# Where weights lie against the moving operand modulo 256 bytes, and 512-column projections by column halves, in an fp32 encoder layer

## Chip, cores and metric

One NeuronCore of one Trainium2 chip. The metric is the device time of one execution in microseconds; the kernel before has a median of 2016.3 us over three runs (2015.68 to 2016.89).

## What is computed

One post-norm layer of a bidirectional encoder over 512 tokens of width 2048, all in float32:

```
h  = layer_norm(x)
z  = h @ w_in                         # 2048 x 3136: latents c_q, c_kv, k_pe, and x_lru, g_lru
ya = attention of 8 heads from the latents (w_uq, w_ukv, rotary, softmax over 512 keys)
yl = gelu(g_lru) * bidirectional RG-LRU(conv(x_lru))     # gates: 8 blocks x 4 products 128x128
h  = layer_norm(alpha*h + concat(ya, yl) @ w_out)        # 2048 x 2048
h  = layer_norm(alpha*h + relu(h @ w_up)^2 @ w_down)     # 2048 x 8192, 8192 x 2048
```

## The kernel before, in words

Activations lie with features on the partitions and the 512 tokens along the free axis. Every fp32 product is made of three fp32r matmuls: weight and activation are each split into a high part (rounded to fp32r, on ACT) and the rest (a subtraction on DVE), and PE adds `wh·xh`, `wh·xl` and `wl·xh` into one PSUM bank. Such a triple is the unit of all that follows. Each matmul loads its 128x128 stationary operand (the weights) while the matmul ahead of it streams its moving operand (the activations): in the trace a `wh·xh` starts at 100.08 us and the load for the matmul behind it at 100.09. So while `wh·xh` streams, `wh` is loaded again; while `wh·xl` streams, `wl` is loaded; while `wl·xh` streams, the next `wh` is loaded.

**Stages in order of time.** The input projections (22 of 25 column tiles by `linear`, L128, each over 16 k-tiles), with the RG-LRU blocks (`lru_block`, L397) between them; attention (`proj`, `q_pe`, `v_pair`, `scores`, `weighted`); the output projection (14 of 16 column tiles by `linear`); the up projection; the down projection. `linear` and the gates of `lru_block` use `mm3` (L123): three matmuls of 512 columns.

**Up and down.** Nearly all of both is `winograd` (L832): seven products (`product`, L816) instead of eight, each of 8 triples of 256 columns, with weights that `wsplit` splits (hi and lo). Its operands are eight blocks of half the tokens: B11, B21, B22, X4, T1, T2, T3 (high part `..h`, rest `..l`). `classic` with `mm_blocks` (L699) does nine column tiles without that scheme, by halves of 256 columns.

**Where weights lie.** `wtile` (L104) makes a slot of 1024 + `WPAD` words, and weights begin `woff` words into it:

```
    WPAD = 32
    woff = [16]
        t = p.tile([P, 1024 + WPAD], F32R, tag=tag, name=tag, bufs=bufs)
        return t[:, woff[0]:woff[0] + 1024]
```

There are three high slots and two low ones in the ring pool `wr`, and one more low slot in `ws_p` that takes every third low part of `winograd`. A slot is 4224 bytes, 128 more than a multiple of 256, so neighbours in the ring differ by 128 modulo 256. Added up over the pools, the high slots begin at 0, 128, 0 modulo 256, the low ones at 128, 0, and the one in `ws_p` at 0; B11, B21 and T2 begin at 128, X4 and B22 at 0, T3 at 192 and T1 at 64 (`pad` puts 16 words ahead of these two, and `woff` is 0 for their weights). All other steps within tiles (a k-tile's 512 bytes of weights, a block's 1024) keep the residue.

**What sets the order.** A scheduler orders the instructions of each engine by the place where they were written; `slab` (L108), which loads and splits one slab of weights (8 k-tiles), is moved up by 100 places (`PO1`). Buffers bound how far a slab can run ahead: three raw, three high, two low.

Of the kernel before, what the change touches and what calls it, by code (L numbers as in the profile page):

```python
# [9 lines left out]
F32 = mybir.dt.float32  # L10
# [38 lines left out]
def body(tc, x, pos, vecs, consts, w_in, w_uq, w_kn, w_v, w_rg, w_out, w_up, w_down, out):  # L49
# [3 lines left out]
    class pool:  # L53
# [6 lines left out]
        def free(self):  # L60
            self.cm.__exit__(None, None, None)
# [9 lines left out]
    def pad(p, n=16):  # L71
        pads[0] += 1
        p.tile([P, n], F32, name=f"pad{pads[0]}_")

    pad_p = pool("pad", "right")
    pad(pad_p, 24)
    cp = pool("const")
    wr = pool("wring")

# [18 lines left out]
        return vec[:, c:c + 1]  # L98


    WPAD = 32
    woff = [16]

    def wtile(p, tag, bufs):  # L104
        t = p.tile([P, 1024 + WPAD], F32R, tag=tag, name=tag, bufs=bufs)
        return t[:, woff[0]:woff[0] + 1024]

    def slab(src, w=1024, dst=None):  # L108
        with tc.high_priority(offset=PO1):
# [13 lines left out]
    def mm3(acc, wh, wl, xh, xl, first, last):  # L123
        T.matmul(acc, wh, xh, start=first, stop=False)  # L124
        T.matmul(acc, wh, xl, start=False, stop=False)  # L125
        T.matmul(acc, wl, xh, start=False, stop=last)  # L126

    def linear(slabs, xh, xl, kts, loaded=None):  # L128

        acc = ps.tile([P, S], F32, tag="mm", name="mm", bufs=3)  # L130
        n = len(kts)
        per = 8
        for s0 in range(0, n, per):
            m = min(per, n - s0)
            wh, wl = loaded[s0 // per] if loaded else slab(slabs[kts[s0] // per], m * P)
            for j in range(m):
                kt = kts[s0 + j]
                mm3(acc, wh[:, j * P:(j + 1) * P], wl[:, j * P:(j + 1) * P], xh[kt], xl[kt],
                    s0 + j == 0, s0 + j == n - 1)
        return acc  # L140

    def split(f, hi, lo):
# [87 lines left out]
    cqh, cql, ckh, ckl = ([lat[n][:, k] for k in range(4)] for n in ("cqh", "cql", "ckh", "ckl"))  # L230
    ctab = cn_p.tile([P, S], F32, name="ctab")
    stab = cn_p.tile([P, S], F32, name="stab")
    KA = cn_p.tile([P, S], F32R, name="KA")
    KB = cn_p.tile([P, S], F32R, name="KB")
    pad(cn_p)

    yl_p = pool("yl", "right")
    ylru = [yl_p.tile([P, S], F32, name=f"ylru{k}") for k in range(8)]
# [157 lines left out]
    def lru_block(b):  # L396
        xp = xps.pop(b)  # L397
        xc = wk.tile([P, S], F32, tag="xc", name="xc", bufs=2)
        V.tensor_scalar(out=xc, in0=xp[:, 0:S], scalar1=col("conv_w", b), scalar2=None, op0=ALU.mult)
        for tap in range(1, 4):  # L400
            V.scalar_tensor_tensor(out=xc, in0=xp[:, tap:tap + S], scalar=col("conv_w", tap * 8 + b),
                                   in1=xc, op0=ALU.mult, op1=ALU.add)
        V.tensor_scalar(out=xc, in0=xc, scalar1=col("conv_b", b), scalar2=None, op0=ALU.add)
        xh = wk.tile([P, S], F32R, tag="xch", name="xch")
        xl = wk.tile([P, S], F32R, tag="xcl", name="xcl")
        split(xc, xh, xl)
        wh, wl = slab(w_rg[b], 512)
        r, i, a = {}, {}, {}
        for d in range(2):
            for g, (dst, bn) in enumerate(((r, "rg_b_a"), (i, "rg_b_i"))):  # L410
                gp = ps.tile([P, S], F32, tag="sc", name="gp", bufs=2)
                j = (2 * d + g) * P
                mm3(gp, wh[:, j:j + P], wl[:, j:j + P], xh, xl, True, True)
                dst[d] = wk.tile([P, S], F32, tag="ri"[g], name="ri", bufs=2)
                A.activation(dst[d], gp, AF.Sigmoid, bias=col(bn, d * 8 + b))
        th = {}
        for d in range(2):
            V.tensor_tensor(out=i[d], in0=i[d], in1=xc, op=ALU.mult)
            th[d] = wk.tile([P, S], F32, tag="th", name="th", bufs=2)
            A.activation(th[d], r[d], AF.Tanh, scale=sp8[:, d * 8 + b:d * 8 + b + 1])  # L420
        for d in range(2):
            a[d] = r[d]
            A.activation(a[d], r[d], AF.Exp, scale=sp8n[:, d * 8 + b:d * 8 + b + 1])
        hd = {}
        for d in range(2):
            a2 = wk.tile([P, S], F32, tag="a2", name="a2", bufs=2)
            A.activation(a2, a[d], AF.Square)
            V.scalar_tensor_tensor(out=th[d], in0=a2, scalar=1.0, in1=th[d], op0=ALU.add, op1=ALU.mult)
        for d in range(2):
            A.activation(th[d], th[d], AF.Sqrt)  # L430
            V.tensor_tensor(out=i[d], in0=i[d], in1=th[d], op=ALU.mult)
            hd[d] = ylru[b] if d == 0 else wk.tile([P, S], F32, tag="hb", name="hb", bufs=2)
            if d == 0:
                V.tensor_tensor_scan(out=hd[d], data0=a[d], data1=i[d], initial=0.0,
                                     op0=ALU.mult, op1=ALU.add)
            else:
                V.tensor_tensor_scan(out=hd[d][:, ::-1], data0=a[d][:, ::-1], data1=i[d][:, ::-1],
                                     initial=0.0, op0=ALU.mult, op1=ALU.add)
        V.tensor_tensor(out=ylru[b], in0=hd[0], in1=hd[1], op=ALU.add)
# [57 lines left out]
    ya_p = pool("ya", "right")  # L497
    yah = [ya_p.tile([P, S], F32R, name=f"yah{k}") for k in range(8)]
    yal = [ya_p.tile([P, S], F32R, name=f"yal{k}") for k in range(8)]
    atw = pool("attnw", "right")  # L500
    pad(atw)
    at = pool("attn", "right")
    woff[0] = 0

    def v_pair(hp):

        vh = atw.tile([P, 4, 256], F32R, tag="vh", name="vh", bufs=2)
        vl = atw.tile([P, 4, 256], F32R, tag="vl", name="vl", bufs=2)
        wh, wl = slab(w_v[hp])
        for t in range(0, 4, 2):  # L510
            acc = ps.tile([P, S], F32, tag="mm", name="mmv", bufs=3)
            for u in range(2):
                sl = slice((t + u) * P, (t + u + 1) * P)
                o = acc[:, u * 256:(u + 1) * 256]
                for k in range(4):
                    ws = slice(k * 256, (k + 1) * 256)
                    T.matmul(o, ckh[k][:, sl], wh[:, ws], start=(k == 0 and u == 0), stop=False)
                    T.matmul(o, ckl[k][:, sl], wh[:, ws], start=False, stop=False)
                    T.matmul(o, ckh[k][:, sl], wl[:, ws], start=False, stop=(k == 3 and u == 1))
            split(acc, vh[:, t:t + 2, :].rearrange("p a b -> p (a b)"),  # L520
                  vl[:, t:t + 2, :].rearrange("p a b -> p (a b)"))
        return vh, vl
# [2 lines left out]

    def q_pe(hp):
        acc = linear([w_uq[8 + hp]], cqh, cql, range(4))
        qo = at.tile([P, S], F32, tag="f", name="qo", bufs=2)
        rotary(acc, qo, at)
        for u in range(2):  # L530
            q = at.tile([P, S], F32R, tag="Q", name="Q", bufs=4)
# [5 lines left out]

    def proj(hd):
        ops = []
        for wsrc, xh, xl, p, n in ((w_uq[hd], cqh, cql, atw, "q"), (w_kn[hd], ckh, ckl, at, "k")):  # L540
            acc = linear([wsrc], xh, xl, range(4))
            hi = p.tile([P, S], F32R, tag=n + "h", name=n + "h", bufs=2)
            lo = p.tile([P, S], F32R, tag=n + "l", name=n + "l", bufs=2)
# [59 lines left out]
    for hd in range(NH):  # L603
# [1 line left out]
            scores(hd + 1)  # L605
        weighted(hd)
        prep(hd + 2)
    pad(atw)
    free(at)
    free(atw)  # L610
    free(cn_p)
    woff[0] = 16


    ta_p = pool("topsA")
# [2 lines left out]
    def op_tiles(p, names):  # L618
        for n in names:
# [3 lines left out]
            opf[n] = p.tile([P, 8, HS], F32, name=n + "l")  # L623
            opl[n] = opf[n].bitcast(F32R)
            if n in ("T3", "T1"):
                pad(p)

    op_tiles(ta_p, ("B11", "B21", "T3"))

# [157 lines left out]
    lon = [0]  # L787

    def wsplit(f, n):
        woff[0] = 0 if n in ("T3", "T1") else 16  # L790
        with tc.high_priority(offset=PO2):
            w = wsplit_(f)
        woff[0] = 16
        return w

    def wsplit_(f):
# [240 lines left out]
```

## Time and profile before

| | |
|---|---|
| median of three runs | 2016.3 us |
| the profiled execution | 2017.38 us |
| its span | 2015.6 us |
| PE busy | 1971.6 us, 98% of the span, 14408 matmuls |
| weight loads (PEld, beside PE) | 1844.7 us |
| DVE busy | 1506.3 us, 75% |
| ACT busy | 1012.4 us, 50% |
| granted TensorE clock | 0.997 |

A matmul's duration in the profile holds its way through the array, and neighbours overlap: what a matmul costs in a stream is the distance from its start to the next one's start, which the timeline shows to 0.01 us. Over a product of 24 matmuls or a column tile of 48 this gives the cost of one to well under a nanosecond.

### The profile page before, as it was taken

How to read it: one execution, taken by the hardware profiler on the slowest of the kernel's cores; microseconds unless marked ns; L12 is line 12 of the kernel's file. 1: busy time of each engine (PE TensorE's matmuls, PEld its weight loads, DVE VectorE, ACT ScalarE, POOL GpSimd, SP SyncE). 2: the span in 40 equal slices, each digit the busy share in tenths (PEclk: the TensorE clock that was granted, in tenths of full speed). 3: DMA queues.
4: the chain of work that ended last, by engine and by line, in shares of the span. 5: the costliest groups of instructions: out<-in, count | busy, mean ns of one | idle time of the engine just before them, and what ended most of it. 6: DMA issues, size and time to landing. Idle time of an engine off the chain costs nothing.

```text
span 2015.6 us, 35154 instructions
## 1 busy us (share of the span) xinstructions
PE 1971.6 (98%) x14408; PEld 1844.7 (92%) x14408; DVE 1506.3 (75%) x2150; ACT 1012.4 (50%) x1482; POOL 11.5 (1%) x17
## 2 busy tenths in 40 slices
PE   6999999999999999999999999999999999999997
PEld 6778778787788899999999999999999999999996
DVE  7565655777333697888878888888898888889885
ACT  6565566555222455555555555566363454445453
POOL 1000000000000000000000000000000000000000
PEclk9999999999999999999999999999999999999999
DMA  7232232222333445444454544586364355346332
GB/s 255 78 96 91 89 94 84 58 58 67 112 110 115 138 166 173 157 158 168 149 179 146 175 152 163 168 279 217 112 220 158 105 183 193 106 138 239 103 98 84
DMA packets 113873, 283.93 MB, mean 141 GB/s; under 512 B 10160, under 2 KB 56368, under 8 KB 109616
## 3 DMA queue, kind: packets, MB, share of 16 engines
q1 hardware_dynamic: 113712, 281.68, 43.0%
q8 instruction: 113, 1.85, 0.4%
q14 instruction: 48, 0.39, 0.1%
HBM read 234.19 MB, written 46.14 MB: 139 GB/s over the span
## 4 chain that ended last, share of the span: by engine, by line
PE 90%; DVE 3%; DMA 2%; ACT 2%; issue 2%; POOL 0%; SPq 0%; POOLq 0%; ACTq 0%; DVEq 0%
PE st_mm L822 8%; PE st_mm L821 8%; PE st_mm L823 8%; PE mm L126 7%; PE mm L125 7%; PE mm L124 7%; PE st_tr L822 5%; PE st_tr L821 5%; PE st_tr L823 5%; PE st_sc L821 5%; PE st_sc L822 5%; PE st_sc L823 5%; PE mm L706 2%; PE mm L707 2%; PE mm L708 1%
## 5 line engine op out<-in xcount | busy, mean ns | idle before, releaser
L143 ACT ACTIVATE whi<-raw 128x1024 fp32r<-128x1024 f32 x399 | 422.6, 1060 | 546.4 <-DVE raw L826 249.3
L144 DVE TENSOR_TENSOR wlo<-raw,whi 128x1024 fp32r<-128x1024 f32 x399 | 487.2, 1223 | 147.0 <-ACT whi L143 135.0
L826 DVE TENSOR_TENSOR raw<-raw 128x1024 f32<-128x1024 f32 x228 | 278.4, 1221 | 3.6
L120 DVE TENSOR_TENSOR wlo<-raw,whi 128x1024 fp32r<-128x1024 f32 (+1 forms) x128 | 141.4, 1106 | 173.0 <-PE mm L126 118.4
L119 ACT ACTIVATE whi<-raw 128x1024 fp32r<-128x1024 f32 (+1 forms) x128 | 123.5, 966 | 209.5 <-PE mm L125 158.8
L124 PE MATMUL mm<-hh,whi 128*128 128x512 f32 x352 | 139.4, 396 | 2.4 <-ACT xp L393 2.4
L126 PE MATMUL mm<-hh,wlo 128*128 128x512 f32 x352 | 139.9, 398 | 0.4 <-DVE wlo L120 0.4
L125 PE MATMUL mm<-hl,whi 128*128 128x512 f32 x352 | 139.3, 396 | 0.0
L821 PE MATMUL st_tr<-B22h,whi 128*128 128x256 f32 x456 | 128.2, 281 | 1.7 <-ACT whi L143 1.7
L821 PE MATMUL st_sc<-X4h,whi 128*128 128x256 f32 x456 | 127.5, 280 | 1.2 <-ACT s L843 1.2
L822 PE MATMUL st_tr<-B22l,whi 128*128 128x256 f32 x456 | 128.0, 281 | 0.0
L821 PE MATMUL st_mm<-T2h,whi 128*128 128x256 f32 x456 | 127.5, 280 | 0.4 <-ACT whi L143 0.4
L822 PE MATMUL st_mm<-T2l,whi 128*128 128x256 f32 x456 | 127.8, 280 | 0.0
L823 PE MATMUL st_tr<-B22h,wlo 128*128 128x256 f32 x456 | 127.7, 280 | 0.0
L821 PE MATMUL st_mm<-B21h,whi 128*128 128x256 f32 x456 | 127.4, 279 | 0.3 <-ACT s L840 0.3
L822 PE MATMUL st_tr<-T1l,whi 128*128 128x256 f32 x456 | 127.6, 280 | 0.0
L822 PE MATMUL st_mm<-B21l,whi 128*128 128x256 f32 x456 | 127.6, 280 | 0.0
L822 PE MATMUL st_sc<-T3l,whi 128*128 128x256 f32 x456 | 127.6, 280 | 0.0
L823 PE MATMUL st_sc<-T3h,wlo 128*128 128x256 f32 x456 | 127.3, 279 | 0.2 <-DVE wlo L144 0.2
L822 PE MATMUL st_sc<-X4l,whi 128*128 128x256 f32 x456 | 127.4, 279 | 0.0
L822 PE MATMUL st_mm<-B11l,whi 128*128 128x256 f32 x456 | 127.2, 279 | 0.0
L821 PE MATMUL st_tr<-T1h,whi 128*128 128x256 f32 x456 | 127.2, 279 | 0.0
(439 smaller groups left out, 5948.4 us busy)
## 6 DMA issues: line engine op xcount, KB each, us to landing
raw<-in_w_up SPq DMA_DIRECT2D x128, 512.0 KB, 3.8
raw<-in_w_down SPq DMA_DIRECT2D x128, 512.0 KB, 4.0
u_dram<-uo SPq DMA_DIRECT2D x32, 1024.0 KB, 3.9
raw<-in_w_in SPq DMA_DIRECT2D x50, 512.0 KB, 3.5
raw<-in_w_out SPq DMA_DIRECT2D x32, 512.0 KB, 3.5
X4l<-u_dram SPq DMA_DIRECT2D x18, 512.0 KB, 5.1
x<-in_x SPq DMA_DIRECT2D x8, 512.0 KB, 7.2
h_dram<-hf SPq DMA_DIRECT2D x32, 128.0 KB, 2.2
```

Source lines behind the costliest of these rows:

```text
L119: A.activation(hi[:, :w], raw[:, :w], AF.Copy)
L120: V.tensor_tensor(out=lo[:, :w], in0=raw[:, :w], in1=hi[:, :w].bitcast(F32), op=ALU.subtract)
L124: T.matmul(acc, wh, xh, start=first, stop=False)
L125: T.matmul(acc, wh, xl, start=False, stop=False)
L126: T.matmul(acc, wl, xh, start=False, stop=last)
L143: A.activation(hi, f, AF.Copy)
L144: V.tensor_tensor(out=lo, in0=f, in1=hi.bitcast(F32), op=ALU.subtract)
L706: T.matmul(o, wh[:, ws], oph[b][:, j], start=first and t == 0, stop=False)
L821: T.matmul(acc, wh[:, ws], oph[n][:, j], start=first and j == 0, stop=False, **sk)
L822: T.matmul(acc, wh[:, ws], opl[n][:, j], start=False, stop=False, **sk)
L823: T.matmul(acc, wl[:, ws], oph[n][:, j], start=False, stop=j == 7, **sk)
L826: V.tensor_tensor(out=o, in0=x, in1=y, op=op)
```

## The change

Weight slots are 1088 words, 4352 bytes, a multiple of 256, so that every slot has the same residue. High parts begin 16 words into their slot and low parts 48; for operands that lie 64 bytes on (T3, T1) 32 and 0; for the gates, whose operand lies elsewhere, the two are exchanged. Pads are resized to match, the pool of attention's weights `atw` is merged into `at`, and `qo` has one buffer instead of two. `linear` and the gates call `mm3h`, which makes the three matmuls of each k-tile for the first 256 columns and then again for the other 256. `mm3` stays in `weighted` and in the two places that work on half the tokens.

```diff
     pad_p = pool("pad", "right")
-    pad(pad_p, 24)
+    pad(pad_p, 56)
...
-    WPAD = 32
-    woff = [16]
+    WPAD = 64
+    FAR = (16, 48)
+    woff = [FAR]

     def wtile(p, tag, bufs):
         t = p.tile([P, 1024 + WPAD], F32R, tag=tag, name=tag, bufs=bufs)
-        return t[:, woff[0]:woff[0] + 1024]
+        o = woff[0][tag == "wlo"]
+        return t[:, o:o + 1024]
...
+    def mm3h(acc, wh, wl, xh, xl, first, last):
+
+        for t in range(2):
+            c = slice(t * 256, (t + 1) * 256)
+            T.matmul(acc[:, c], wh, xh[:, c], start=first and t == 0, stop=False)
+            T.matmul(acc[:, c], wh, xl[:, c], start=False, stop=False)
+            T.matmul(acc[:, c], wl, xh[:, c], start=False, stop=last and t == 1)
...
-                mm3(acc, wh[:, j * P:(j + 1) * P], wl[:, j * P:(j + 1) * P], xh[kt], xl[kt],
-                    s0 + j == 0, s0 + j == n - 1)
+                mm3h(acc, wh[:, j * P:(j + 1) * P], wl[:, j * P:(j + 1) * P], xh[kt], xl[kt],
+                     s0 + j == 0, s0 + j == n - 1)
...
+    pad(cn_p, 48)
     KA = cn_p.tile([P, S], F32R, name="KA")
     KB = cn_p.tile([P, S], F32R, name="KB")
-    pad(cn_p)
...
+        woff[0] = FAR[::-1]
         wh, wl = slab(w_rg[b], 512)
+        woff[0] = FAR
...
-                mm3(gp, wh[:, j:j + P], wl[:, j:j + P], xh, xl, True, True)
+                mm3h(gp, wh[:, j:j + P], wl[:, j:j + P], xh, xl, True, True)
...
-    atw = pool("attnw", "right")
-    pad(atw)
     at = pool("attn", "right")
-    woff[0] = 0
+    woff[0] = (32, 0)
...
-        qo = at.tile([P, S], F32, tag="f", name="qo", bufs=2)
+        qo = at.tile([P, S], F32, tag="f", name="qo")
...
             if n in ("T3", "T1"):
-                pad(p)
+                pad(p, 48)
...
-        woff[0] = 0 if n in ("T3", "T1") else 16
+        woff[0] = (32, 0) if n in ("T3", "T1") else FAR
```

**PE, first k-tiles of an output column tile** (`mm` is the PSUM bank, `ylh`/`yll` the moving operand's parts). Before:

```order
L124 MATMUL mm<-ylh_4650,whi 128x512 x2
L125 MATMUL mm<-yll_4651,whi 128x512
L126 MATMUL mm<-ylh_4650,wlo 128x512
L124 MATMUL mm<-ylh_4654,whi 128x512
L125 MATMUL mm<-yll_4655,whi 128x512
L126 MATMUL mm<-ylh_4654,wlo 128x512
```

With the change:

```order
L134 MATMUL mm<-ylh_6036,whi 128x256 x2
L135 MATMUL mm<-yll_6037,whi 128x256
L136 MATMUL mm<-ylh_6036,wlo 128x256
L134 MATMUL mm<-ylh_6036,whi 128x256
L135 MATMUL mm<-yll_6037,whi 128x256
L136 MATMUL mm<-ylh_6036,wlo 128x256
L134 MATMUL mm<-ylh_6040,whi 128x256
```

Each k-tile is now six matmuls of 256 columns, the weights are loaded for each, and the triple has the form that `product` has.

**ACT, the first RG-LRU block** (`ri` and `th`, `a` are the block's gates and decay, `gp` their PSUM bank, `whi<-raw` the split of a slab of projection weights). Before:

```order
L415 ACT_TABLE_LOAD
L415 ACTIVATE ri<-gp,vec 128x512 x2
L420 ACTIVATE th<-ri,sp_845 128x512
L415 ACTIVATE ri<-gp,vec 128x512
L119 ACTIVATE whi<-raw 128x1024
L415 ACTIVATE ri<-gp,vec 128x512
L420 ACTIVATE th<-ri,sp_845 128x512
L423 ACT_TABLE_LOAD
L423 ACTIVATE ri<-ri,sp8n 128x512 x2
L427 ACTIVATE a_924<-ri 128x512
L427 ACTIVATE a_927<-ri 128x512
L119 ACTIVATE whi<-raw 128x1024
```

With the change:

```order
L427 ACT_TABLE_LOAD
L427 ACTIVATE ri<-gp,vec 128x512 x2
L432 ACTIVATE th<-ri,sp_845 128x512
L427 ACTIVATE ri<-gp,vec 128x512 x2
L432 ACTIVATE th<-ri,sp_845 128x512
L435 ACT_TABLE_LOAD
L435 ACTIVATE ri<-ri,sp8n 128x512 x2
L439 ACTIVATE a_936<-ri 128x512
L439 ACTIVATE a_939<-ri 128x512
L121 ACTIVATE whi<-raw 128x1024
```

The slab's split that stood between the gates now stands behind the whole chain: a k-tile is six instructions instead of three, so that 100 places reach half as far in the work of PE. The other seven blocks moved alike. The order of the transfers on SP moves by single places, POOL's not at all.

## Rows read from the trace of the kernel before

**Rows 1.** The page: busy time by engine, and the group of winograd's low parts.

```profile
PE 1971.6 (98%) x14408; PEld 1844.7 (92%) x14408; DVE 1506.3 (75%) x2150; ACT 1012.4 (50%) x1482; POOL 11.5 (1%) x17
...
L144 DVE TENSOR_TENSOR wlo<-raw,whi 128x1024 fp32r<-128x1024 f32 x399 | 487.2, 1223 | 147.0 <-ACT whi L143 135.0
```

**Rows 2.** Stretches: length, busy by engine, PEclk, DMA share, GB/s.

```profile
860.12:1095.61 235.49, 235.49 (x2019) 235.49 (x2017) 193.22 (x228) 124.70 (x204) 0.00 (x0) 1.00 0.48 161
...
60.00:504.00 444.00, 434.17 (x2031) 349.92 (x2029) 285.11 (x505) 253.19 (x391) 2.03 (x2) 1.00 0.26 78
```

**Rows 3.** Timeline of PE, up projection, first matmul of each product: start, length.

```profile
843.14 0.28 PE L821 MATMUL st_mm<-T2h,whi 128*128 128x256 f32 x1
...
846.00 0.28 PE L821 MATMUL st_mm<-B11h,whi 128*128 128x256 f32 x1
...
848.75 0.28 PE L821 MATMUL st_sc<-T3h,whi 128*128 128x256 f32 x1
...
860.12 0.28 PE L821 MATMUL st_tr<-B22h,whi 128*128 128x256 f32 x1
...
862.84 0.28 PE L821 MATMUL st_mm<-T2h,whi 128*128 128x256 f32 x1
...
865.58 0.28 PE L821 MATMUL st_mm<-B11h,whi 128*128 128x256 f32 x1
...
868.30 0.28 PE L821 MATMUL st_sc<-T3h,whi 128*128 128x256 f32 x1
...
873.78 0.28 PE L821 MATMUL st_sc<-X4h,whi 128*128 128x256 f32 x1
...
1095.61 0.28 PE L821 MATMUL st_tr<-B22h,whi 128*128 128x256 f32 x1
```

**Rows 4.** The same, down projection.

```profile
1544.13 0.28 PE L821 MATMUL st_mm<-B11h,whi 128*128 128x256 f32 x1
...
1602.86 0.28 PE L821 MATMUL st_mm<-B11h,whi 128*128 128x256 f32 x1
```

**Rows 5.** The same, `classic`: first and last matmul of two column tiles.

```profile
1341.22 0.28 PE L706 MATMUL mm<-B11h,whi 128*128 128x256 f32 x1
...
1363.37 0.28 PE L708 MATMUL mm<-B22h,wlo 128*128 128x256 f32 x1
```

**Rows 6.** The same, two input column tiles: first and last matmul of each.

```profile
270.29 0.40 PE L124 MATMUL mm<-hh,whi 128*128 128x512 f32 x1
...
281.26 0.39 PE L126 MATMUL mm<-hh,wlo 128*128 128x512 f32 x1
281.49 0.39 PE L124 MATMUL mm<-hh,whi 128*128 128x512 f32 x1
...
292.31 0.39 PE L126 MATMUL mm<-hh,wlo 128*128 128x512 f32 x1
```

**Rows 7.** The same, output projection on half the tokens (`mm3`, 256 columns).

```profile
674.07 0.28 PE L124 MATMUL mmh<-ylh,T3h 128*128 128x256 f32 x1
...
678.90 0.28 PE L126 MATMUL mmh<-yah,T3l 128*128 128x256 f32 x1
```

**Rows 8.** Timeline of ACT, an RG-LRU block.

```profile
148.74 0.69 ACT L415 ACTIVATE ri<-gp,vec 128x512 f32<-128x512 f32 x1
149.30 0.73 ACT L420 ACTIVATE th<-ri,sp 128x512 f32<-128x512 f32 x1
150.05 1.28 ACT L423 ACT_TABLE_LOAD   x1
151.34 0.72 ACT L423 ACTIVATE ri<-ri,sp8n 128x512 f32<-128x512 f32 x1
151.97 1.04 ACT L119 ACTIVATE whi<-raw 128x1024 fp32r<-128x1024 f32 x1
152.92 0.71 ACT L423 ACTIVATE ri<-ri,sp8n 128x512 f32<-128x512 f32 x1
153.53 1.14 ACT L427 ACTIVATE a<-ri 128x512 f32<-128x512 f32 x2
```

More of the change, by code (lines that the diff above doesn't have):

```diff
@@ L499, in body @@
     yal = [ya_p.tile([P, S], F32R, name=f"yal{k}") for k in range(8)]
-    atw = pool("attnw", "right")
-    pad(atw)
     at = pool("attn", "right")
-    woff[0] = 0
+    woff[0] = (32, 0)
     def v_pair(hp):
-        vh = atw.tile([P, 4, 256], F32R, tag="vh", name="vh", bufs=2)
-        vl = atw.tile([P, 4, 256], F32R, tag="vl", name="vl", bufs=2)
+        vh = at.tile([P, 4, 256], F32R, tag="vh", name="vh", bufs=2)
+        vl = at.tile([P, 4, 256], F32R, tag="vl", name="vl", bufs=2)
+        woff[0] = (0, 0)
         wh, wl = slab(w_v[hp])
+        woff[0] = (32, 0)
         for t in range(0, 4, 2):
@@ L539, in proj @@
         ops = []
-        for wsrc, xh, xl, p, n in ((w_uq[hd], cqh, cql, atw, "q"), (w_kn[hd], ckh, ckl, at, "k")):
+        for wsrc, xh, xl, p, n in ((w_uq[hd], cqh, cql, at, "q"), (w_kn[hd], ckh, ckl, at, "k")):
             acc = linear([wsrc], xh, xl, range(4))
@@ L607, in body @@
         prep(hd + 2)
-    pad(atw)
     free(at)
-    free(atw)
     free(cn_p)
-    woff[0] = 16
+    woff[0] = FAR
     ta_p = pool("topsA")
@@ L789, in wsplit @@
     def wsplit(f, n):
-        woff[0] = 0 if n in ("T3", "T1") else 16
+        woff[0] = (32, 0) if n in ("T3", "T1") else FAR
         with tc.high_priority(offset=PO2):
             w = wsplit_(f)
-        woff[0] = 16
+        woff[0] = FAR
         return w
```

## The prediction

> **What bounds the kernel now.** I read the page first: PE is busy 98% of the span, ACT and DVE far less [rows 1]. The stretches say the same where most of the time goes: in the up projection PE is busy all of 235.49 us at a granted clock of 1.00, the full 2.4 GHz, with DVE at 193.22; between 60 and 504 us it is busy 434.17 of 444.00 [rows 2]. So time is gained only where matmuls follow each other faster, and the third view, the timeline of PE, says how fast they do. The reader is to look at one thing there: products that compute the same take different times. T2 takes 846.00 - 843.14 = 2.86 us at one place and 865.58 - 862.84 = 2.74 at another; B11 takes 848.75 - 846.00 = 2.75 and 868.30 - 865.58 = 2.72 [rows 3]. Nothing waits in them, the clock is the same, the operands are the same tiles. What differs is the slot of the ring that the weights lie in.
>
> I call distance the address of the weights being loaded less that of the moving operand being streamed, modulo 256: one for the high weights against the moving operand, one for the low. With the residues that the section on the kernel lists, the first T2 has (high 192, low 64), the second (64, 192); the B11 at 846.00, the B22 at 860.12, and T3 and T1 from 868.30 have (64, 192) as well. Following the slots through the 399 products [rows 1], 103 have (64, 192), 103 have (192, 64), 106 (192, 192) and 87 (64, 64). Products at (64, 192) take 2.72 to 2.77 us almost wherever they stand; at (192, 64) 2.85 to 2.86; the two classes of equal distances mostly 2.83 and now and then 2.72, as the B11 at 865.58, which is (192, 192) behind two products at (64, 192). The four at (64, 192) between 860.12 and 865.58 and between 868.30 and 873.78 take 5.46 + 5.48 = 10.94 us, 2.735 each, 114.0 ns per matmul [rows 3].
>
> **The change, part by part.** *Slots, offsets, pads.* With slots of 4352 bytes every product has (64, 192). Before, 84 products from 860.12 to 1095.61 take 235.49 us, 2.803 each [rows 3], and 21 in the down projection from 1544.13 to 1602.86 take 58.73, 2.797 [rows 4]; 2.80 for all. The gain is 399 x (2.800 - 2.735) = **25.9 us**, all on the path, since PE is never idle in that stretch [rows 2]. Bounds: at best all go at 2.72, as the B22 at 860.12 [rows 3], 31.9 us; at worst nothing, if the distance is not the cause. I take 2.735, the mean of neighbours that were all at (64, 192). DVE covers its part: 193.22 us for 84 products is 2.30 each [rows 2], still below 2.735; were that cover gone, a product would take DVE's 2.30, so nothing is lost there.
>
> *Classics.* Four passes from 1341.22 to 1363.37 are 191 steps in 22.15 us, 116.0 ns each [rows 5]. Their halves lie at opposite distances before and both at (64, 192) after: 9 column tiles x 96 = 864 matmuls x (116.0 - 114.0) = **1.7 us**.
>
> *Halves.* `linear` and the gates have 352 + 224 + 48 + 32 + 32 = 688 k-tiles (input, output, q, k, gates), 2064 matmuls of 512 columns. One input tile takes 10.97 us for 47 steps, 233.4 ns, the next 10.82, 230.2 ns [rows 6]; with the middle, 231.8, they cost 478.4 us. After it is 4128 matmuls of 256 columns at (64, 192). No row shows this stage in halves; the nearest is the product at (64, 192), the same triple with the same two loads of `wh`: 4128 x 114.0 = 470.6, a gain of **7.8 us**. Bounds: at 2.72 us per product, 113.3 ns, 10.7 gained; at the 117.8 ns of the output projection on half the tokens (41 steps in 4.83 us [rows 7]), whose distances are equal, 4128 x 117.8 = 486.3, 7.9 lost. The doubled loads lie under the matmuls ahead, as in the products, where a load per 256 columns leaves PE busy throughout [rows 2].
>
> *Order around the RG-LRU.* Splitting doubles the instructions of a k-tile, so the slab's head start of 100 places covers half the work, and ACT now splits a slab behind a block's whole chain instead of within it. From the last gate's matmul that chain is 0.69 + 0.73 + 1.28 + 0.72 + 0.71 + 1.14 + 1.04 = 6.3 us up to the slab's high part [rows 8], and 1.2 more on DVE for the low one [rows 1]: 7.5. In the changed order PE has 79 to 85 matmuls of 256 columns (9.0 us or more at 114.0) between the last gate and the slab's first use in six of the eight blocks; 68 (7.8 us) in one, which just covers it; and 47 (5.4 us) in the first, which leaves a wait of **2 us** there. On ACT `xp`, and on DVE the scans, stand behind that split; both have slack as long as the slab's wait stays that short. Bounds: nothing, if the first block waits anyway, to 8 x 1.5 = 12 us, if other work on ACT eats the 1.5 us of margin in every block.
>
> *The rest* I cost at nothing: the one buffer of `qo` is written again two heads later; the pool merge and pads move no work; SP's order moves by single places; the 256 matmuls of 512 columns that stay whole in attention change distance, which by the spread of 3.2 ns between the two tiles is at most 0.8 us either way [rows 6].
>
> **Sum.** 25.9 + 1.7 + 7.8 - 2.0 = 33.4 us. The profiled execution took 2017.4 (span 2015.6 and 1.8 around it): 1984.0 for one like it. The median stands 1.1 below it, so 1982.9; I say **1983**.
>
> Two rules of the Trainium skill speak against this. The page "SBUF — State Buffer", section "Who interferes with whom", gives TensorE two independent read ports, one for the moving operand and one for weight loads, and says that it waits on nobody; by that the slot could not matter and the first two terms would be 0. The trace disagrees: 2.86 against 2.74 us for one product [rows 3]. The page "TensorE: Matmul & The Clock Gate", section "Back-to-back issue gap", adds about 2.5 ns to each warm matmul whatever its length; by it the 2064 additional ones would cost an estimated 5.2 us where I count a gain of 7.8.
>
> **The rivals.** *Halves don't pay* (0.10). The products' rate could belong to their stage, and halves run between the classics' 116.0 ns, 478.8 us, no gain [rows 5], and 117.8, 7.9 us lost [rows 7]: 1991 to 1999. For it: no row has halves there. Against: classics, products and 512-column tiles all follow the distances.
>
> *Late weights* (0.06). The split behind the LRU chain costs in every block, the 12 us above or somewhat more: 1990 to 2000. For it: the margin is 1.5 us; against: buffers already bound the head start, and PE is busy 98% there [rows 2].
>
> *Slots don't matter, slower* (0.05). If the rate of a product came from its stage's other traffic, in step with the ring by accident, products and classics stay, and the halves, which then go at the products' mean of 2.80/24 = 116.7 ns, cost 481.7 - 478.4 = 3.3 us; with the wait of 2.0 this is 2016.3 + 5.3 = 2022. That is also what the first page above would leave. Against it stand both T2 and the same behaviour of four products in a row.
>
> *The wrong pairing, slower* (0.02). The change may not do what it says: were the operands 128 bytes, one pad, off what the offsets suppose, all would have (192, 64), 2.86 us a product. 399 x 0.06 + 864 x 3.2 ns + 4128 x 119.2 ns - 478.4 + 2.0 = 23.9 + 2.8 + 13.7 + 2.0 = 42 us: 2059. It decides from that one slip on; the pool sizes added up speak against it.
>
> **How the numbers follow.** The forecast has 0.76, within 1974 to 1990; the remaining 0.01 is open. The low end is the best rate everywhere without a wait, 2016.3 - (31.9 + 2.3 + 10.7) = 1971, nearly; the range of 1974 to 1993 takes in the forecast and the near part of the first two rivals. Faster by over 0.2% (4 us, about what a measurement of this kernel can tell from no change): 0.76 + 0.10 + 0.06 = 0.92. Slower: 0.05 + 0.02, less 0.01 for a loss too small to tell: 0.06. Same: 0.02.
>
> **What would show it.** Right: every product 2.72 to 2.75 us with no class of 2.83 or 2.86 left, 84 of them in 230 us; an input tile of 96 halves in 10.9 us; one wait of some 2 us in the first RG-LRU block. Wrong: products at two rates still; halves at 116 ns or more; a wait of PE on `whi` or `wlo` in each block; PE busy below 97% in the stretch of products, which would make another engine the bound.

## The result, and the profile after

| | before | changed |
|---|---|---|
| median of four runs each | 2015.99 us (2014.41 to 2016.89) | 1985.11 us (1981.93 to 1988.03) |
| the profiled execution, its span | 2017.38, 2015.6 us | 1981.93, 1980.2 us |
| granted TensorE clock | 0.997 | 0.997 |

The ratio is 0.9847, interval 0.983 to 0.9865: faster by 1.5%. The forecast was 1983.0, range 1974 to 1993. A second comparison of the same two kernels gave 0.985 (0.9831 to 0.9869; `after_again` below). The profiled execution of the changed kernel is the quickest of its four, so by the two profiles the gain is 35.4 us, by the medians 30.9.

The page of the changed kernel, busy time and winograd's low parts. PE has the same share of a shorter span; DVE's work is what it was [rows 1].

```profile
PE 1932.5 (98%) x16472; PEld 1898.9 (96%) x16472; DVE 1501.9 (76%) x2150; ACT 1015.2 (51%) x1482; POOL 11.7 (1%) x17
...
L154 DVE TENSOR_TENSOR wlo<-raw,whi 128x1024 fp32r<-128x1024 f32 x399 | 484.7, 1222 | 127.5 <-ACT whi L153 121.7
```

A stretch of the changed kernel: 84 products from a T1 to a T1 (columns as in [rows 2]).

```profile
826.28:1055.24 228.96, 228.96 (x2019) 228.96 (x2017) 191.92 (x228) 124.93 (x205) 0.00 (x0) 1.00 0.47 166
```

The same number of products took 235.49 us [rows 2]. PE was busy all the time before and after, at the same clock: only the distance from matmul to matmul changed. The timeline of PE, up projection of the changed kernel, first matmul of each of seven products in a row, answers to [rows 3]:

```profile
834.46 0.28 PE L831 MATMUL st_tr<-B22h,whi 128*128 128x256 f32 x1
...
837.17 0.28 PE L831 MATMUL st_mm<-T2h,whi 128*128 128x256 f32 x1
...
839.89 0.28 PE L831 MATMUL st_mm<-B11h,whi 128*128 128x256 f32 x1
...
842.62 0.28 PE L831 MATMUL st_sc<-T3h,whi 128*128 128x256 f32 x1
...
845.36 0.28 PE L831 MATMUL st_tr<-T1h,whi 128*128 128x256 f32 x1
...
848.08 0.28 PE L831 MATMUL st_sc<-X4h,whi 128*128 128x256 f32 x1
...
850.82 0.28 PE L831 MATMUL st_mm<-B21h,whi 128*128 128x256 f32 x1
```

T2 takes 2.72 us, B11 2.73, T3 2.74, T1 2.72, X4 2.74. The same holds through both stages. Counted from a product's first matmul to the start of PE's next instruction behind it, 272 of the 399 products take 2.72 or 2.73 us and 108 take 2.74; the other 19 (2.81 to 4.16) hold waits, stand behind a wait or have other work between. The classes of 2.82 to 2.86, 258 products before, are gone. The 2.74 is T3 and X4 alone: there the moving operand's residue changes, so the first matmul of the product streams beside a load at another distance. T3 and T1 lie 64 bytes on and so do their weights: T1 takes the 2.72 us of the others at the same distances with both operands at other places, so the distance counts and not the weights' place by itself.

The column tiles in halves, first matmul of two neighbouring input tiles (answers to [rows 6]), and the first and last matmul of four passes of `classic` (answers to [rows 5]):

```profile
269.12 0.28 PE L134 MATMUL mm<-hh,whi 128*128 128x256 f32 x1
...
280.00 0.28 PE L134 MATMUL mm<-hh,whi 128*128 128x256 f32 x1
...
1320.08 0.28 PE L716 MATMUL mm<-B11h,whi 128*128 128x256 f32 x1
...
1341.73 0.28 PE L718 MATMUL mm<-B22h,wlo 128*128 128x256 f32 x1
```

A tile of 96 halves takes 10.88 us, 113.3 ns each, and the classic goes at 21.65 / 191 = 113.4 ns where it had 116.0.

**Where the 35.4 us come from**, by the starts of the first matmul of each stage: input projections from the first matmul of `linear` 279.2 to 277.9 us (-1.3), attention 160.3 to 160.4 (+0.1), output projection to its half-token tiles 163.3 to 162.5 (-0.8), up projection from its first product 593.5 to 575.6 (-17.9), down projection 626.7 to 612.7 (-14.0), the rest -1.5. In the two long stages the 399 products, start to start and with all waits, fell from 1125.9 to 1095.7 us (-30.2), and the classics from 100.6 to 98.7 (-1.9).

### The profile page after: what moved, and what is told of

It is laid out like the page before. It is cut to its first block, busy times and chain, and to the rows that moved or that the text cites. A ratio compares the mean times of both kernels' runs of the same rounds, so it can differ in the third digit from the quotient of the medians.

```text
span 1980.2 us, 39293 instructions
## 1 busy us (share of the span) xinstructions
PE 1932.5 (98%) x16472; PEld 1898.9 (96%) x16472; DVE 1501.9 (76%) x2150; ACT 1015.2 (51%) x1482; POOL 11.7 (1%) x17
## 4 chain that ended last, share of the span: by engine, by line
PE 87%; DVE 4%; ACT 3%; DMA 3%; issue 2%; POOL 0%; SPq 0%; POOLq 0%; DVEq 0%; ACTq 0%
PE st_mm L831 8%; PE st_mm L832 8%; PE st_mm L833 8%; PE mm L136 7%; PE mm L135 7%; PE mm L134 7%; PE st_sc L831 5%; PE st_sc L833 5%; PE st_tr L833 5%; PE st_tr L831 5%; PE st_tr L832 5%; PE st_sc L832 5%; PE mm L716 1%; PE mm L718 1%; PE mm L717 1%
## 5 line engine op out<-in xcount | busy, mean ns | idle before, releaser
L134 PE MATMUL mm<-hh,whi 128*128 128x256 f32 x704 | 195.4, 278 | 2.6 <-ACT xp L403 1.8
L136 PE MATMUL mm<-hh,wlo 128*128 128x256 f32 x704 | 195.6, 278 | 0.8 <-DVE wlo L122 0.8
L135 PE MATMUL mm<-hl,whi 128*128 128x256 f32 x704 | 196.0, 278 | 0.0
L134 PEld LDWEIGHTS mm<-hh,whi 128*128 128x128 f32 x704 | 132.9, 189 | 3.0 <-ACT xp L403 2.0
L136 PEld LDWEIGHTS mm<-hh,wlo 128*128 128x128 f32 x704 | 132.9, 189 | 1.0 <-DVE wlo L122 1.0
L135 PEld LDWEIGHTS mm<-hl,whi 128*128 128x128 f32 x704 | 133.0, 189 | 0.0
L833 PE MATMUL st_sc<-X4h,wlo 128*128 128x256 f32 x456 | 126.2, 277 | 0.0
L831 PE MATMUL st_sc<-T3h,whi 128*128 128x256 f32 x456 | 126.1, 277 | 0.0
L833 PE MATMUL st_tr<-T1h,wlo 128*128 128x256 f32 x456 | 126.1, 276 | 0.0
L833 PE MATMUL st_mm<-B11h,wlo 128*128 128x256 f32 x456 | 126.0, 276 | 0.0
```

Source lines behind the costliest of these rows:

```text
L134: T.matmul(acc[:, c], wh, xh[:, c], start=first and t == 0, stop=False)
L135: T.matmul(acc[:, c], wh, xl[:, c], start=False, stop=False)
L136: T.matmul(acc[:, c], wl, xh[:, c], start=False, stop=last and t == 1)
L831: T.matmul(acc, wh[:, ws], oph[n][:, j], start=first and j == 0, stop=False, **sk)
L833: T.matmul(acc, wl[:, ws], oph[n][:, j], start=False, stop=j == 7, **sk)
```

## The experiments

In these, a pair like (64, 192) is the distance of the high weights and of the low ones, as in the prediction. The ratio is always to the kernel before on the same chip.

### e1_whole and e2_halves: the two parts of the change, each alone

`e1_whole` has the new slots and offsets, without the halves; `e2_halves` is the kernel before with the halves alone.

```diff
 # e1_whole, against the changed kernel (linear and the gates)
-                mm3h(acc, wh[:, j * P:(j + 1) * P], wl[:, j * P:(j + 1) * P], xh[kt], xl[kt],
+                mm3(acc, wh[:, j * P:(j + 1) * P], wl[:, j * P:(j + 1) * P], xh[kt], xl[kt],
 # e2_halves, against the kernel before (linear and the gates)
-                mm3(acc, wh[:, j * P:(j + 1) * P], wl[:, j * P:(j + 1) * P], xh[kt], xl[kt],
+                mm3h(acc, wh[:, j * P:(j + 1) * P], wl[:, j * P:(j + 1) * P], xh[kt], xl[kt],
```

> The changed kernel with its slots and offsets, but every projection in whole matmuls of 512 columns again (no halves). Theory (the distance of weight loads to the streamed operand sets the rate of 256-column matmuls): products all at 2.73 us as in the changed kernel, 30 us gained there and 2 in the classics; the projections stay near 232 ns per 512 columns and the order around the RG-LRU is the old one, so 1984 to 1989 us. Rival (the halves carry the gain, the slots little): 2005 us or more, with products at 2.83 us.

> The kernel before with halves alone: its old slots, which put the halves at all four pairs of distances. Theory: products stay at a mean of 2.80 us; the halves go at the same mixture, 116.7 ns on average, 481 us instead of 478, and the first RG-LRU block waits 2 us: 2017 to 2023 us. Rival (halves pay by themselves, whatever the distance): 113.7 ns each, 2004 to 2010 us.

Measured: `e1_whole` 1985.43 us, ratio 0.9858 (0.9842 to 0.9874); `e2_halves` 2022.08, ratio 1.0042 (1.0027 to 1.0057), a loss. The stretch of 84 products in `e1_whole` and then in `e2_halves`:

```profile
827.25:1056.21 228.96, 228.96 (x2019) 228.96 (x2018) 191.97 (x228) 124.91 (x205) 0.00 (x0) 1.00 0.48 167
```

```profile
842.52:1078.01 235.49, 235.49 (x2018) 235.49 (x2017) 193.21 (x228) 124.69 (x204) 0.00 (x0) 1.00 0.45 162
```

These are the 228.96 us of the changed kernel and the 235.49 of the kernel before, to 0.01 us. In `e2_halves` the halves run at 115.2 ns in the mean, for the old slots give them all four pairs. So the slots bring the gain, 29 us; the halves alone lose 8 us and beside the slots bring 0.3 us by the medians, which the intervals don't tell from nothing.

Matmuls of 512 columns keep their mean in `e1_whole`, 231.8 ns. But the slots move them too: in the kernel before, one slab of eight k-tiles takes from 228.9 to 233.5 ns per matmul (the two tiles of [rows 6] are 233.4 and 230.2), in `e1_whole` the undisturbed input tiles all take 231.7 to 231.9. That is a range of 2%, where 256 columns have 5% (113.3 to 119.1), and in the kernel before it averages out.

### e3_swap, e4_near, e5_zero, e6_half: other distances, everything else as in the change

Only the numbers of `woff` differ. For most operands, with the gates and T3, T1 and attention to match:

```diff
-    FAR = (16, 48)
+    FAR = (48, 16)    # e3_swap: (192, 64) everywhere
+    FAR = (16, 16)    # e4_near: (64, 64) everywhere
+    FAR = (0, 32)     # e5_zero: (0, 128) everywhere
+    FAR = (32, 0)     # e6_half: (128, 0) everywhere
```

> The changed kernel with the two offsets exchanged, so that every triple has distances (high 192, low 64) instead of (64, 192); nothing else differs. Theory: all products 2.85 us (50 us more than the changed kernel), classics and halves at 119 ns (4.5 and 21 us more): 2055 to 2065 us. Rival (it is enough that the high and the low part differ by 128 and every slot is the same): as the changed kernel, 1981 to 1989 us.

> The changed kernel with high and low weights at the same distance, (64, 64). Theory (equal distances keep the pace with which a stream begins, fast or slow): products at either 2.72 or 2.83 us with nothing between, in an order that repeats, and a time between 1980 (all fast) and 2038 (all slow), about 2010 if as mixed as in the kernel before. Rival (only the high part's distance of 64 counts): all products at 2.73 us and 1981 to 1989 us.

Measured: `e3_swap` 2001.25 us, ratio 0.9937 (0.9922 to 0.9951); `e4_near` 2004.91, ratio 0.995 (0.9936 to 0.9965). The first lies 12 us above what the rival said and 54 below what the theory said. Its timeline of PE, up projection, first matmuls of the first three products:

```profile
757.71 0.28 PE L831 MATMUL st_mm<-B11h,whi 128*128 128x256 f32 x1
...
760.56 0.28 PE L831 MATMUL st_sc<-T3h,whi 128*128 128x256 f32 x1
...
763.31 0.28 PE L831 MATMUL st_tr<-T1h,whi 128*128 128x256 f32 x1
```

B11 takes 2.85 us and T3 2.75, both at (192, 64); after them all products up to 1315.85 us take 2.72 or 2.73, at the very pair that took 2.85 to 2.86 throughout before. In all 354 products take 2.72 or 2.73 and 21 take 2.85. In the input projections of the same kernel nearly all halves run at 118.9 ns; in the output projection they are slow from the second tile up to about 583 us and at 113.3 behind it. So (192, 64) does not fix the pace. What the rows show is that a stream at this pair **keeps** the pace that it has: the classic ahead of 757.71 ran at 118.8 ns, the first B11 took that over, and within T3, where the residue jumps, it became 113.3 and stayed so until the next wait. Not every jump frees the stream: behind the classic at 1491 us B11, T3 and T1 all take 2.85, through the jump into T3, and only X4, behind the jump out of T1, is at 2.74.

`e4_near`, the same place, five products in a row:

```profile
751.47 0.28 PE L831 MATMUL st_mm<-B11h,whi 128*128 128x256 f32 x1
...
754.19 0.28 PE L831 MATMUL st_sc<-T3h,whi 128*128 128x256 f32 x1
...
757.01 0.28 PE L831 MATMUL st_tr<-T1h,whi 128*128 128x256 f32 x1
...
759.84 0.29 PE L831 MATMUL st_sc<-X4h,whi 128*128 128x256 f32 x1
...
762.58 0.28 PE L831 MATMUL st_mm<-B21h,whi 128*128 128x256 f32 x1
```

All five are at (64, 64), and B11 takes 2.72, T3 and T1 2.82 and 2.83, X4 2.74. The pattern repeats in most of the 57 groups of seven (T1 is at 2.83 in 54 of them, X4 at 2.74 in 52, T2 and B11 at 2.72 or 2.73 in 47 and 49): there the jump into T3 throws the stream to 117.7 ns, the jump out of T1 brings it back. Equal distances carry either pace too.

> The changed kernel with all weights 64 bytes lower: distances (high 0, low 128) instead of (64, 192), the difference between the two kept. Theory A (only the difference counts: a low part 128 bytes farther than the high one brings a stream back to the fast pace): as the changed kernel, products at 2.72 us, 1981 to 1989 us. Theory B (the 64 and the 192 themselves count): slower, with products at a second pace for long stretches, 1995 to 2040 us.

> The changed kernel with distances (high 128, low 0): the difference of the two again 128, all shifted by 64 from the exchanged pair. Theory A (only the difference counts, and modulo 256 the pair 128 and 0 differs by 128 in the wrong direction, as 192 and 64): as the run with the offsets exchanged, 1997 to 2005 us, with long stretches at 118.9 ns per matmul. Theory B (the distances themselves count): another time, above 2005 us or below 1990.

Measured: `e5_zero` 2057.19 us, ratio 1.0204 (1.0189 to 1.0219); `e6_half` 2050.32, ratio 1.0169 (1.0154 to 1.0185). Two products of each, `e5_zero` first:

```profile
765.28 0.28 PE L831 MATMUL st_mm<-B11h,whi 128*128 128x256 f32 x1
...
768.14 0.28 PE L831 MATMUL st_sc<-T3h,whi 128*128 128x256 f32 x1
```

```profile
763.98 0.28 PE L831 MATMUL st_mm<-B11h,whi 128*128 128x256 f32 x1
...
766.82 0.28 PE L831 MATMUL st_sc<-T3h,whi 128*128 128x256 f32 x1
```

2.86 and 2.84 us, and there is no quicker product in either: at these two pairs, even multiples of 64, every product is slow, in spite of the same waits and jumps that bring others back. `e5_zero` is 17 us beyond what its theory B allowed, which expected slow stretches and not slow products throughout. That the two distances differ by 128 is not enough, then: in the products the quick pace was seen at odd multiples of 64 alone, and only (64, 192) returned to it by itself. `e5_zero`, slow throughout, is what the prediction's rival of the wrong pairing described, and lands at that rival's 2059.

Between the changed kernel and `e5_zero` nothing differs but four pairs of offsets, and 72 us. The Trainium skill, page "SBUF — State Buffer", section "Who interferes with whom", gives TensorE separate read ports for weights and moving operand and lets it wait for nobody. The trace disagrees in this: 2.72 against 2.86 us for the same product says that where the two operands lie against each other matters.

### e8_even: (192, 64) without the jumps

If a stream at (192, 64) keeps its pace, and the jumps at T3 and T1 are what frees it, then without jumps it should stay slow once it is slow.

```diff
 # against e3_swap: T3 and T1 at the residue of the others
-                pad(p)
+                pad(p, 64)
...
-                pad(p, 48)
+                pad(p, 64)
...
-        woff[0] = (0, 32) if n in ("T3", "T1") else FAR
+        woff[0] = FAR
```

> The run with the offsets exchanged (192, 64), and T3 and T1 moved to the residue of the other operands, so that no product begins with a jump of the distance. Theory (a stream keeps its pace, fast or slow; at (64, 192) it goes back to the fast one within a product, at (192, 64) it does not, and there only the jumps at T3 and T1 brought it back; waits and the transposes between tiles make it slow): once slow, products stay at 2.85 us, so far more than the 20 slow products of the run with the jumps, up to all 399, 2010 to 2055 us. Rival (the jumps have no part in it; products are mostly fast at any fixed pair): 1997 to 2004 us as with the jumps.

Measured: 2011.09 us, ratio 0.9978 (0.9957 to 0.9999), and the executions differ widely: 1999.49 to 2019.93 over ten, a spread of 20 us where `e3_swap` has 5 and the kernel before 5 in that comparison (2012.83 to 2018.13). The profiled one took 2006.37. Its timeline of PE in the down projection:

```profile
1478.65 0.39 PE L831 MATMUL st_sc<-X4h,whi 128*128 128x256 f32 x1 [0.76 <-ACT s L853]
...
1481.60 0.28 PE L831 MATMUL st_mm<-B21h,whi 128*128 128x256 f32 x1
...
1484.45 0.28 PE L831 MATMUL st_tr<-B22h,whi 128*128 128x256 f32 x1
```

Up to here nearly all its products took 2.72 us. Then PE waits 0.76 us for ACT, and with that the stream has the slow pace: 2.85 for B21, and so on for 53 products in a row, to 1653 us. After the classic that follows there they take 2.72 again. This is the kept pace without anything that resets it, and the spread between executions is what one would expect where each wait falls a little differently. It fits; that each execution's time follows its waits is not shown, since only one of the ten has a trace.

### e7_ahead: the slabs' head start doubled

The halves make a head start of 100 places reach half as far. This gives it 200 everywhere.

```diff
-PO1, PO2 = 100, 100
+PO1, PO2 = 200, 100
```

> The changed kernel with a slab's head start of 200 places instead of 100, which halves had cut to half the work. Theory (the first RG-LRU block waits some 2 us for weights that ACT splits behind its chain): the two waits of 1 us each at 79 to 81 us are gone, the rest is as in the changed kernel: 1981 to 1986 us, at most 3 us less. Rival (the wait has another cause, or the deeper queue on ACT delays the chain itself): the waits stay or come back elsewhere, no gain or some us lost.

Measured: 1988.64 us, ratio 0.9864 (0.9845 to 0.9883); the expected gain did not come. The waits in the first RG-LRU block are gone, but the list of PE's waits has new ones in the classic ahead of the products (waited for, us in total, times, longest):

```profile
PE mm L717 <- DVE B22l L154: 3.7, 4, 1.6
```

All classics together take 107 us where they took 98.7. DVE splits the weights' slabs, which are moved up by the same number everywhere, as well as B22; that the slabs now stand ahead of B22 there is the likely reading, and `e9_mend` below bears on it.

### after_again and e9_mend: the head start in `linear` alone, and another order in `v_pair`

```diff
-    def slab(src, w=1024, dst=None):
-        with tc.high_priority(offset=PO1):
+    def slab(src, w=1024, dst=None, ahead=PO1):
+        with tc.high_priority(offset=ahead):
...
-            wh, wl = loaded[s0 // per] if loaded else slab(slabs[kts[s0] // per], m * P)
+            wh, wl = loaded[s0 // per] if loaded else slab(slabs[kts[s0] // per], m * P, ahead=200)
...
-        woff[0] = (0, 0)
+        woff[0] = (0, 32)
...
-                    T.matmul(o, ckl[k][:, sl], wh[:, ws], start=False, stop=False)
-                    T.matmul(o, ckh[k][:, sl], wl[:, ws], start=False, stop=(k == 3 and u == 1))
+                    T.matmul(o, ckh[k][:, sl], wl[:, ws], start=False, stop=False)
+                    T.matmul(o, ckl[k][:, sl], wh[:, ws], start=False, stop=(k == 3 and u == 1))
```

> The changed kernel itself, to stand beside the next one on one chip: 1982 to 1988 us. Every theory says the same.

> The changed kernel with the head start of 200 places for the slabs of the projections alone (not of the up and down projection), and with the values' products in the order and at the distances (64, 192). Theory (the first RG-LRU block waits 2 us on late weights; the values' products lie at equal distances and run at 118 ns): 2 us and 192 x 4.5 ns = 0.9 us less than the changed kernel, 1979 to 1986 us; the wait at 79 to 81 us is gone and the classics keep no new wait. Rival (the head start moves other work of ACT out of its place, as for the up projection): no gain.

Measured: `after_again` 1984.12 us, ratio 0.985 (0.9831 to 0.9869), with the same two waits in the first block; `e9_mend` 1981.92, ratio 0.9836 (0.9818 to 0.9855), without them and without `e7_ahead`'s new ones in the classic. The 2.2 us are about what the waits cost, but the intervals overlap: a version better than the changed kernel is not shown. (The trace of `e9_mend`, its slowest execution, has a wait of 2.2 us in one product for a low part from DVE.)

The second edit missed. `v_pair`'s products, 192 matmuls in which the activations are the stationary operand, take 22.65 us in `e9_mend` and 22.6 in the changed kernel, where they took 21.8 before. In the changed kernel, first matmul of a run of 48 and the last of it:

```profile
348.96 0.28 PE L529 MATMUL mmv<-whi,ckh 128*128 128x256 f32 x1
...
354.50 0.28 PE L531 MATMUL mmv<-wlo,ckh 128*128 128x256 f32 x1
```

5.54 us over 47 steps is 117.9 ns. It goes with the halves: `e1_whole`, with the same slots and offsets, has 113.8 ns and 21.8 us there, `e2_halves`, with the old slots, 22.6. So at the same distances either pace is kept, again; but it is not the pace of the stream ahead, which ran at 113.3 ns up to the first of the 48. The change of operands sets it, and what decides between the two is not shown. With (64, 192) it did not turn to 113.3. The pairs that are quick elsewhere have the streamed operands at one residue; here the two streamed parts, `wh` and `wl`, lie at different ones. Whether that is the reason was not tried.

### e10_late_halves and e11_late_whole: what the transposes take from the halves

The 14 whole output tiles are each followed by four transposes (`to_tokens`, L170), which land in the middle of the next tile's matmuls. Both kernels move them behind the loop; the first has halves, the second (from `e1_whole`) whole 512 columns.

```diff
         V.scalar_tensor_tensor(out=r[n], in0=hres, scalar=ALPHA, in1=acc, op0=ALU.mult, op1=ALU.add)
+    for n in range(KT - NL):
         to_tokens(r[n], st1, n)
```

> The changed kernel with the statistics' transposes of the output projection's first 14 column tiles made behind the last of them, not between. Theory (halves give back at each interruption by transposes what they gain, since a matmul beside transposes takes some 0.3 us whatever its columns): without interruptions the 14 tiles take 14 x 96 x 113.4 ns = 152.4 us, against 155.6 for whole matmuls in the next run, 3 us apart instead of the 0.9 with the transposes between. Rival (the halves' gain is lost elsewhere in the stage): the two stay within 1.5 us.

> The same for the kernel with the new slots and whole matmuls of 512 columns: the 14 column tiles in 14 x 48 x 231.6 ns = 155.6 us by the theory, 3 us more than with halves; within 1.5 us of it by the rival.

Measured, one execution each: 1987.2 us and 1985.91. First and last matmul of the 14 tiles, with halves and whole:

```profile
502.75 0.51 PE L134 MATMUL mm<-ylh,whi 128*128 128x256 f32 x2 [1.20 <-ACT ylh L153]
...
655.65 0.28 PE L136 MATMUL mm<-yah,wlo 128*128 128x256 f32 x1
```

```profile
501.43 0.51 PE L126 MATMUL mm<-ylh,whi 128*128 128x512 f32 x1 [1.20 <-ACT ylh L153]
...
657.44 0.39 PE L128 MATMUL mm<-yah,wlo 128*128 128x512 f32 x1
```

152.9 against 156.0 us: undisturbed, the halves gain 3.1 us in this stage. With the transposes between, the stage takes 162.5 us in the changed kernel and 163.4 in `e1_whole`: 0.9. The whole time shows no gain from the move: the transposes then stand in a row behind, and the half-token tiles with them take 34.8 us where they took 30.1.

One such interruption, in the changed kernel and then in the kernel before:

```profile
584.22 0.28 PE L135 MATMUL mm<-yll,whi 128*128 128x256 f32 x1
584.54 0.66 PE L170 MATMUL tr<-ident,R 128*128 128x128 f32 x4
584.96 0.36 PE L136 MATMUL mm<-ylh,wlo 128*128 128x256 f32 x1
585.16 0.28 PE L134 MATMUL mm<-ylh,whi 128*128 128x256 f32 x1
```

```profile
586.74 0.40 PE L126 MATMUL mm<-ylh,wlo 128*128 128x512 f32 x1
587.04 0.66 PE L160 MATMUL tr<-ident,R 128*128 128x128 f32 x4
587.45 0.48 PE L124 MATMUL mm<-ylh,whi 128*128 128x512 f32 x1
587.77 0.39 PE L125 MATMUL mm<-yll,whi 128*128 128x512 f32 x1
```

From the matmul ahead of the transposes to the one after the next it is 0.94 us with halves and 1.03 with 512 columns. Taking off two matmuls at their own pace (2 x 0.113 and 2 x 0.232) leaves 0.71 and 0.57: the matmul ahead of the transposes takes 0.3 us and the one behind 0.2 to 0.3 whether it streams 256 columns or 512. The interruption costs the halves 0.14 us more.

## Why the prediction was right, and where not

**Products** (25.9 us forecast, 30.2 found). The cause held: where the weights lie, not the stage, sets the time of a product; `e1_whole` has the gain without the halves, `e5_zero` takes it away and more. The term was sized too small. The prediction took 2.735 us, the mean of four neighbours at (64, 192), for all; but three of the four (T2, T3, T1) were at 2.74, with changes of the operand's residue from block to block, and in the new layout only T3 and X4 lie behind such a change. The mean is 228.96 / 84 = 2.726, close to the bound of 2.72. The 2.800 before was a shade low as well: 2.803 in the long stretch.

**Classics** (1.7 forecast, 1.9 found): right, and the stretch went to 113.4 ns where 114.0 were counted.

**Halves** (7.8 forecast, 5.8 with the wait; 0.3 found by the medians of `e1_whole` and the changed kernel, 1.2 by their stages as below): this term of the sum was mis-sized. The rate was right: 113.3 ns in the input tile above, 113.8 in the mean of all undisturbed halves, where 114.0 were counted. What was left out is what stands between the tiles. In the output stage the whole tiles' 672 matmuls of 512 columns at 231.7 ns become 1344 at 113.35, 3.4 us less; but the 29 matmuls that stand beside transposes or waits took 2.27 us beyond their pace before and 4.57 now, which gives 2.3 of it back: the stage is 0.9 us shorter than in `e1_whole`. In the input stage the same excess is 10.4 us against 5.6 in `e1_whole`. Of these 4.8 us 1.9 are the new wait and 1.5 no cost of the halves at all: from 64.75 to 67.50 us, behind a wait of 1.8 us for ACT, PE ran at a granted clock of 0.50, that is 1.2 GHz; the kernel before does so too at that place, `e1_whole` does not. In attention `v_pair` loses 0.8 us, and the whole stage takes 160.4 us against 159.4. The prediction costed the doubled loads as hidden, rightly, and forgot that an interruption has a price per occasion, not per column.

Stretches at the lower clock come at other places in other executions of the same kernel. `after_again` has none at 65 us, but one at 501.70, behind a wait of 1.2 us (the granted clock is the third number from the end):

```profile
501.70:504.90 3.20, 3.20 (x16) 3.20 (x16) 2.70 (x5) 1.32 (x3) 0.00 (x0) 0.50 0.03 7
```

There a half takes 213 ns. So the input stage takes 276.1 us in `after_again` and 277.9 in the changed kernel's first profile, the output stage 164.1 and 162.5: a difference of 1 us between two single profiles of a stage says little until the clock is compared. Without such stretches the halves take 276.1 against 277.5 in `e1_whole` in the input stage (-1.3), 1.0 more in attention and 0.9 less in the output stage: 1.2 us gained.

**The wait in the first RG-LRU block** (2 us forecast): right in place and size. The end of ACT's chain, and PE behind it:

```profile
74.83 0.72 ACT L432 ACTIVATE th<-ri,sp 128x512 f32<-128x512 f32 x1
75.56 1.28 ACT L435 ACT_TABLE_LOAD   x1
76.86 1.34 ACT L435 ACTIVATE ri<-ri,sp8n 128x512 f32<-128x512 f32 x2
78.10 1.14 ACT L439 ACTIVATE a<-ri 128x512 f32<-128x512 f32 x2
79.15 1.04 ACT L121 ACTIVATE whi<-raw 128x1024 fp32r<-128x1024 f32 x1
```

```profile
79.18 0.28 PE L136 MATMUL mm<-hh,wlo 128*128 128x256 f32 x1
80.24 0.39 PE L134 MATMUL mm<-hh,whi 128*128 128x256 f32 x1 [0.79 <-ACT whi L121]
80.46 0.28 PE L135 MATMUL mm<-hl,whi 128*128 128x256 f32 x1
81.50 0.38 PE L136 MATMUL mm<-hh,wlo 128*128 128x256 f32 x1 [0.76 <-DVE wlo L122]
```

The slab's high part ends at 80.19, PE starts at 80.24, and waits again for the low part: two steps of 1.06 and 1.04 us where 0.11 each would do, 1.9 us. In the other seven blocks PE waits for no slab, as forecast.

**The rest at nothing**: nearly. `v_pair` lost the 0.8 us that are counted above with the halves. The output projection on half the tokens went from 117.8 ns [rows 7] to 4.65 / 41 = 113.4:

```profile
671.35 0.28 PE L126 MATMUL mmh<-ylh,T3h 128*128 128x256 f32 x1
...
676.00 0.28 PE L128 MATMUL mmh<-yah,T3l 128*128 128x256 f32 x1
```

This is not to be put down to the change: in `after_again`, the same kernel, the same 41 steps take 4.83 us, 117.8 ns. At equal distances one kernel can have either pace at one place in two executions.

**The sum**: 33.4 forecast, 35.4 by the profiles and 30.9 by the medians. Products came out some 4 us better and the halves 4.5 to 5.5 worse, so that the total hides two errors of opposite sign: that it came so close is in part luck.

**One statement behind the terms was wrong**: that products at (192, 64) take 2.85 to 2.86. In the kernel before they met a stream at the slow pace; `e3_swap` has 354 products at that pair at 2.72 or 2.73. The rival of the wrong pairing, 2059 us, would have been 2001. It had no weight in the forecast, since (64, 192) was read rightly as the pair that is quick wherever it stands.

**The rivals.** *Slots don't matter* fell: the loss it foresaw for the halves alone, though, is there (2022.08 in `e2_halves`, 7.5 us above the kernel before on its chip; 5.3 by the rival's sum). *Halves don't pay* was nearer to the truth than its chance of 0.10: not because of the pace, as it supposed, but by the interruptions and `v_pair`; its time of 1991 to 1999 missed because the products gave more. *Late weights* fell: one block waits, not eight.

**What is left open.** The runs show three paces of 256-column matmuls in this kernel: 113.3 ns, about 117.8 (equal distances) and 118.3 to 119.1. At (64, 192) a stream is back at 113.3 within a product of any wait, `v_pair` apart; at (64, 64) and (192, 64), as the runs show, and by the kernel before at (192, 192) too, it keeps the pace that it has, and waits, transposes and jumps of the residue change it, though not each time; at (0, 128) and (128, 0) it is always slow. That the period is 256 bytes follows from the slots: at 4352 bytes neighbours differ by 256 modulo 512, and all run alike. What in the chip makes it so, why `v_pair` does not follow, and which distances give 512 columns their 228.9 ns, no run here tells.

## What to carry to other kernels

Where PE is busy throughout and the same product takes different times at different places, read the starts of matmuls to 0.01 us and sort them by the residue of the operands' addresses before looking at any engine: here four numbers of padding were worth 1.5%, and the wrong four cost 2%. One layout in which a stream recovers by itself is worth more than one that is quick only as long as nothing disturbs it: here the latter spread over 20 us in ten executions (`e8_even`), the changed kernel over 6 in four. And when a matmul is cut into shorter ones, count what interrupts the stream: here an interruption by transposes cost 0.71 us with 256 columns and 0.57 with 512, so short matmuls, whose gain is a few ns each, lose by it, and everything that is measured in instructions (a slab's head start) shrinks by the same factor. Before two profiles are compared to 1 us, compare their granted clocks stretch by stretch.

## What the runs showed of the hardware that was not expected

- A stream of matmuls keeps a pace for long: 53 products in a row at 2.85 us or more behind a wait of 0.76 us (`e8_even`, 174 us), then 2.72 for the same pair of distances. At that pair, with no jumps of the residue, ten executions of one kernel spread over 20 us.
- Two matmuls of 256 columns take 2 x 113.3 = 226.7 ns, one of 512 takes 231.7, each with its own load of weights. By the Trainium skill, page "TensorE: Matmul & The Clock Gate", section "Back-to-back issue gap", a matmul of N columns, taken by itself, is followed after N / 2.4 + 2.5 ns, which makes two halves the longer way, an estimated 2 x 109.2 against 215.8; the page says itself that a stream of loads and matmuls departs from it, and the prediction used it for a stream. At (64, 192) this case's trace disagrees; at the slow pace (2 x 119 = 238) the halves are the longer way, so here the sign depends on the distance.
- Matmuls of 512 columns depend on the slots too, but less: slabs at 228.9 to 233.5 ns per matmul in the kernel before, undisturbed tiles at 231.7 to 231.9 with the new slots (`e1_whole`).
